# Weight sums moved from GpSimd to VectorE, four planned latencies and half of the embedding evictions changed in a one-core encoder layer

## The chip, the core and the metric

One of the eight cores of a Trainium2 chip runs the whole layer as one program. The engines that matter are TensorE (PE in the profile; its weight loads are listed apart as PEld), VectorE (DVE), ScalarE (ACT), GpSimd (POOL) and SyncE (SP), which issues all DMA transfers of this kernel. Each engine works through its own list of instructions in order and waits on semaphores. The metric is the device time of one execution in microseconds (us).

## The reference, cut to what matters

```python
def layer(x, p, pre_g, w_in, sink, ln_g, ln_b, ws, bs, w_out, post_g, w_pe, w_pg):
    h = rms_norm(x, pre_g)
    z = h @ w_in                                    # 2048 -> 5632
    q, k, v, g_attn, u, vg, g_gmlp = jnp.split(z, IN_SPLITS, axis=-1)
    q, k = rope(q), rope(k)
    a = window_attention(q, k, v, sink) * jax.nn.silu(g_attn)
    m = spatial_gating(gelu(u), gelu(vg), ln_g, ln_b, ws, bs) * jax.nn.silu(g_gmlp)
    y = jnp.concatenate([a, m], axis=-1) @ w_out    # 2048 -> 2048
    x = x + rms_norm(y, post_g)
    return x + jax.nn.sigmoid(x @ w_pg) * (p @ w_pe)
```

It is applied to two sequences of 1024 and 512 tokens, 1536 tokens together, in float32.

## The kernel before

**Products.** The three large products are cut into five sweeps: "a", "b" and "c" make the columns of w_in, "y" those of w_out, "p" those of w_pg. A sweep takes the 1536 tokens in two halves of 768 and the 2048 inputs in two halves of 1024, and multiplies by Strassen's scheme: seven products, in the order 3, 5, 7, 1, 4, 2, 6 (`ORDER`), stand for eight. Product `pr` of weight tile `i` is one pass of TensorE: 8 operand tiles times 2 column blocks of 384 times 3 matmuls. The 3 are there because every float32 value is split in two parts that TensorE takes at full rate, a high part (a copy by ScalarE) and a low part (a difference by VectorE), and high*high, high*low and low*high are added up (`mm3`, lines 174 to 176). There are 266 passes.

**What a pass needs.** For five of the seven products the weight of a pass is a sum or difference of two quarters of the weight matrix. `make_weights` loads both quarters (SyncE, into pool `wrp` of four buffers), adds them on GpSimd (lines 155 and 158 are the helpers `add` and `sub` that record the instruction), and `split_to` makes the high part on ScalarE (line 166) and the low part on VectorE (line 158). Such a sum is 128x1024 elements; there are 190. Names are built alike: `wra4_7` is the raw weight quarter (wr) of sweep a, product 4, tile 7, and `wta4_7` the split weight (wt) made of it; the profile drops the numbers. The operands are `ar` (raw), `a` (split): `ara`, `aa` in sweep a, `arc`, `ac` in sweep c. `psa` to `psp` are the PSUM tiles of the passes, two banks-pairs that take turns, so pass i+2 can start only when pass i has been taken out. `leave_product` takes a pass out of PSUM and adds it to the running outputs `u`, `v`, `o`, on VectorE and ScalarE. At the end of one product the eight operands of the next are split, one after another, while the last pass runs.

**Beside the passes.** `embed` multiplies p by w_pe first (16 tiles j, two halves h, PSUM tiles `pspe`); `leave_pe` copies each out on VectorE (line 397) and stores it. Meanwhile x is squared and summed (`accx`, `sq`) for the first norm, and the first operands are made of it (`x0_normed`, line 440). `rope` turns q and k with three multiplications, one of them on GpSimd, and an addition on GpSimd. `attention` runs 12 blocks of tokens times 2 groups of heads one after another between the matmuls of sweeps b and c: `attend_qk` splits q and k (`qs`, `ks`), the scores are taken (`s`), VectorE and ScalarE make the probabilities `p`, `turn` transposes them (`t`) and splits them (`pt`), `weigh` multiplies them with `vs` (`o`).

**What sets the order.** Nothing is decided on the chip. The program is recorded by a planner (`Line`): each job is a generator that records some instructions and yields how many microseconds it expects until its next step can run; the planner's clock advances with the matmuls recorded (0.1733 us each), and a step is recorded when it is due. So a number behind `yield` says how many matmuls are recorded between one step and the next. A number that is too small puts an instruction in its engine's list before its input is there, and the engine waits.

Of the kernel before, what the change touches and what calls it, by code (L numbers as in the profile page):

```python
# [11 lines left out]
AF = mybir.ActivationFunctionType  # L12
# [11 lines left out]
CH = HT // 2  # L24
# [69 lines left out]
def when(done):  # L94
    while not done():
        yield 0.5
# [3 lines left out]
def tile_encoder_layer(ctx: ExitStack, tc: tile.TileContext, xT, pT, wall, pre_g, post_g, sink,  # L100
                       ln_g, ln_b, wsT, bs, cos, sin, mask, out):
    nc = tc.nc
# [19 lines left out]
    def work(name):  # L122
        return wk.tile([P, HT], F32, tag="wk", name=name)

    def four(name, shape=None, dt=F32):
        return s4p.tile(shape or [P, 1024], dt, tag="s4", name=name)
# [5 lines left out]
    def banks(name):  # L132

        return psm.tile([P, 2, T], F32, tag="ps", name=name)

    def side(name):
        return pss.tile([P, T], F32, tag="sd", name=name)
# [4 lines left out]
    def load(dst, src):  # L142
        nc.sync.dma_start(out=dst, in_=src)
# [10 lines left out]
    def add(eng, o, a, b):  # L154
        eng.tensor_tensor(out=o, in0=a, in1=b, op=ALU.add)  # L155

    def sub(eng, o, a, b):
        eng.tensor_tensor(out=o, in0=a, in1=b, op=ALU.subtract)  # L158
# [4 lines left out]
    V, G = nc.vector, nc.gpsimd  # L163

    def split_to(src, hi, lo, us=1.2):
        nc.scalar.activation(hi, src, AF.Copy)  # L166
        yield us
        sub(V, lo, src, hi.bitcast(F32))

    def halves(t):  # L170
        return t.rearrange("p (c x) -> p c x", c=2)

    def mm3(ps, l, r, start, stop, us):
        nc.tensor.matmul(ps, lhsT=l[0], rhs=r[0], start=start, stop=False)  # L174
        nc.tensor.matmul(ps, lhsT=l[0], rhs=r[1], start=False, stop=False)  # L175
        nc.tensor.matmul(ps, lhsT=l[1], rhs=r[0], start=False, stop=stop)  # L176
        line.spend(3 * us)
# [18 lines left out]
    def load_w(dst, f, h):  # L196

        if f[0] == "c":
            load(dst, wall[f[1], :, h * 1024:(h + 1) * 1024])
            return  # L200
        for i in range(2):
            src = wall[f[1] + 2 * h + i].rearrange("p (k n) -> p k n", k=4)
            load(dst[:, i * 512:(i + 1) * 512].rearrange("p (k n) -> p k n", k=4),
                 src[:, :, f[2]:f[2] + P])
# [10 lines left out]
    def make_weights(j, sw, pr, i):  # L215

        nm = f"{sw.name}{pr}_{i}"
        sign, *quarters = B_OF[pr]
        rs = []
        for kh, n in quarters:  # L220
            r = wrp.tile([P, 1024], F32, tag="wr", name=f"wr{nm}_{n}{kh}")
            load_w(r, sw.pairs[i][n][0], kh)
            rs.append(r)
        yield 9.0
        if sign:
            (add if sign > 0 else sub)(G, rs[0], rs[0], rs[1])
            yield 3.5
        yield from when(lambda: passes[0] >= j - 2)
        w = wtp.tile([P, 2, 1024], F32R, tag="wt", name=f"wt{nm}")
        yield from split_to(rs[0], w[:, 0, :], w[:, 1, :])  # L230
        weights[j] = w
# [162 lines left out]

    def leave_pe(j, h, ps):
        o = arp.tile([P, HT], F32, tag="ar", name=f"pe{j}_{h}")
        V.tensor_copy(out=halves(o), in_=ps[:, :, 0:CH])
        yield 1.6
        store(pe_d[j][h], o)

# [174 lines left out]
    def span_of(n):  # L575
        lo, hi = (0, 8) if n < 8 else (8, 12)
        return max(lo, n - 1), min(hi, n + 2)

    def attend_qk(g, n, into):
        b0, b1 = span_of(n)  # L580
        w = (b1 - b0) * P
        nm = f"{g}_{n}"
        h, off = n // HB, (n % HB) * P
        r = [work(f"aq{nm}"), work(f"ak{nm}")]
        load(r[0][:, 0:512].rearrange("p (i t) -> p i t", i=4),
             q_d[g][h][:, :, off:off + P].rearrange("i p t -> p i t"))
        load(r[1][:, 0:w], k_d[g][:, b0 * P:b1 * P])
        yield 9.0
        q = four(f"qs{nm}", [P, 2, 512], F32R)
        ks = four(f"ks{nm}", [P, 2, 512], F32R)  # L590
        nc.scalar.activation(q[:, 0, :], r[0][:, 0:512], AF.Copy)
        nc.scalar.activation(ks[:, 0, 0:w], r[1][:, 0:w], AF.Copy)
        yield 0.8
        sub(V, q[:, 1, :], r[0][:, 0:512], q[:, 0, :].bitcast(F32))
        yield 0.6
        sub(V, ks[:, 1, 0:w], r[1][:, 0:w], ks[:, 0, 0:w].bitcast(F32))
        yield 3.0
        into.append((q, ks))

    def attend_v(g, n, into):  # L600
        b0, b1 = span_of(n)
        w = (b1 - b0) * P
        nm = f"{g}_{n}"
        r = work(f"av{nm}")
        load(r[:, 0:w].rearrange("p (b d) -> p b d", b=b1 - b0), v_d[g][b0:b1].rearrange("b p d -> p b d"))
        yield 9.0
        vs = four(f"vs{nm}", [P, 2, 512], F32R)
        yield from split_to(r[:, 0:w], vs[:, 0, 0:w], vs[:, 1, 0:w], 0.8)
        yield 0.8
        into.append(vs)  # L610

    def attend(g, n, got):

        b0, b1 = span_of(n)
        m0 = (b0 - n + 1) * P
        nb = b1 - b0
        w = nb * P
        nm = f"{g}_{n}"
        h, off = n // HB, (n % HB) * P
        yield from when(lambda: got)  # L620
        q, ks = got.pop()
        mx = small.tile([P, 4], F32, tag="mx", name=f"mx{nm}")
        sm = small.tile([P, 4], F32, tag="sm", name=f"sm{nm}")
        es = small.tile([P, 4], F32, tag="es", name=f"es{nm}")
        gv = []
        line.spawn(attend_v(g, n, gv), 1.0)
        ss, ps_ = [], []

        def reduce(i):
            hd = 4 * g + i  # L630
            p = pp.tile([P, 3 * P], F32, tag="p", name=f"p{nm}_{i}")
            V.tensor_tensor_reduce(out=p[:, 0:w], in0=ss[i][:, 0:w], in1=mask_sb[:, m0:m0 + w],
                                   op0=ALU.add, op1=ALU.min, scale=-SCALE,
                                   scalar=nsink[:, hd:hd + 1], accum_out=mx[:, i:i + 1])
            ps_.append(p)

        def expo(i):
            nc.scalar.activation(ps_[i][:, 0:w], ps_[i][:, 0:w], AF.Exp, scale=-1.0, bias=mx[:, i:i + 1],
                                 accum_out=sm[:, i:i + 1])

        for i in range(6):
            if i < 4:
                ss.append(side(f"s{nm}_{i}"))
                mm3(ss[i][:, 0:w], [q[:, x, i * P:(i + 1) * P] for x in range(2)],
                    [ks[:, x, 0:w] for x in range(2)], True, True, w / 2400. + 0.0133)
            if 1 <= i < 5:
                reduce(i - 1)
            if i >= 2:
                expo(i - 2)
            yield 1.0  # L650
        add(V, es, mx, sink_sb[:, 4 * g:4 * g + 4])
        yield 0.3
        nc.scalar.activation(es, es, AF.Exp)
        yield 0.6
        add(V, sm, sm, es)
        V.reciprocal(out=sm, in_=sm)
        yield 0.6
        for i in range(4):
            nc.scalar.activation(ps_[i][:, 0:w], ps_[i][:, 0:w], AF.Copy, scale=sm[:, i:i + 1])
        yield 4.6  # L660
        pts = {}

        def turn(b):
            tp = side(f"t{nm}_{b}")
            for i in range(4):
                nc.tensor.transpose(tp[:, i * P:(i + 1) * P], ps_[i][:, b * P:(b + 1) * P], ident)
            line.spend(0.43)
            yield 0.4
            pt = pts[b] = four(f"pt{nm}_{b}", [P, 2, 512], F32R)
            yield from split_to(tp, pt[:, 0, :], pt[:, 1, :], 0.9)  # L670

        def weigh(b):
            mm3(o, [vs[:, x, b * P:(b + 1) * P] for x in range(2)],
                [pts[b][:, x, :] for x in range(2)], b == 0, b == nb - 1, 0.2266)

        yield from turn(0)
        yield from turn(1)
        yield from when(lambda: gv)
        vs = gv[0]
        yield 2.0  # L680
        o = side(f"o{nm}")
        weigh(0)
        if nb > 2:
            yield from turn(2)
            yield 2.0
        for b in range(1, nb):
            weigh(b)
        yield 0.8
        t = work(f"ao{nm}")
        nc.scalar.activation(t[:, 0:512], o, AF.Copy)  # L690
        yield 1.5
        store(at_d[g][h][:, :, off:off + P].rearrange("i p t -> p i t"),
              t[:, 0:512].rearrange("p (i t) -> p i t", i=4))
        attended.add((g, n))
# [193 lines left out]
    pq.clear()  # L888
    embedded.append(True)
    line.spawn(make_weights(2, *items[2]))  # L890

    j = 0
    for s, (sw, pr) in enumerate(segs):
        n = len(sw.pairs)
        out_of = {5: (1, 0), 4: (0, 0), 2: (0, 1), 6: (1, 1)}.get(pr)
        for i in range(n):
# [12 lines left out]
            ps = banks(f"ps{sw.name}{pr}_{i}")  # L909
# [86 lines left out]
```

## Time and profile before

| | us |
|---|---|
| time, median of 3 runs | 2557.67 (2557.42 to 2560.88) |
| profiled execution, own time | 2555.26 |
| its span, first to last instruction | 2553.5 |
| TensorE busy | 2483.7 (97%) |
| VectorE busy | 1731.8 (68%) |
| ScalarE busy | 966.0 (38%) |
| GpSimd busy | 708.1 (28%) |
| mean granted TensorE clock | 0.992 |

TensorE is busy for 97% of the span and idle for 69.8 us of it. Busy time alone doesn't tell what a change of the other engines is worth: it is to be read from the waits of TensorE, one by one, and from what held the engine that ended each of them.

### The profile page before, as it was taken

To read this page: it belongs to the slowest core of one execution; us is meant where nothing else is said; L and a number is where in the kernel's file an instruction comes from. 1 tells how busy PE (TensorE), PEld (TensorE's weight loads), DVE (VectorE), ACT (ScalarE), POOL (GpSimd) and SP (SyncE) were. 2 spreads that over 40 slices of the span, in tenths; PEclk is the share of its full clock that TensorE was granted. 3 is DMA by queue.
4 is the path that set the end of the run, shared out by engine and by line. 5 is a ranking of instruction groups with operands and counts; after the bars stand their busy time and mean duration, and the time that the engine had idled before them with its cause. 6 is when DMAs were issued, how large, how long until landed. Compare 5 with 4: busy or idle time off the path is not lost.

```text
span 2553.5 us, 36547 instructions
## 1 busy us (share of the span) xinstructions
PE 2483.7 (97%) x14268; PEld 2448.7 (96%) x14268; DVE 1731.8 (68%) x1903; ACT 966.0 (38%) x1386; POOL 708.1 (28%) x300
## 2 busy tenths in 40 slices
PE   7999999999999999999998899999999999999999
PEld 7898999999989999999998899999999999999998
DVE  7659566866676767667767665556577976757775
ACT  3243222224775543333546742332233333322421
POOL 0254334454022102301221013203220331433444
PEclk9999999999999999999999999999999999999999
DMA  8957776667566688878656577567577988879985
GB/s 292 387 197 262 249 238 230 225 211 263 195 225 212 180 270 293 303 248 300 200 173 209 187 273 280 219 215 250 170 245 257 342 313 305 302 251 301 325 315 208
DMA packets 372397, 645.97 MB, mean 253 GB/s; under 512 B 29312, under 2 KB 212096, under 8 KB 372224
## 3 DMA queue, kind: packets, MB, share of 16 engines
q1 hardware_dynamic: 372224, 643.63, 73.9%
q8 instruction: 112, 1.84, 0.3%
q14 instruction: 61, 0.50, 0.1%
HBM read 533.43 MB, written 110.10 MB: 252 GB/s over the span
## 4 chain that ended last, share of the span: by engine, by line
PE 80%; DVE 9%; ACT 4%; issue 3%; DMA 3%; POOL 1%; SPq 1%; DVEq 0%; POOLq 0%; ACTq 0%
PE psy L175 6%; PE psy L176 6%; PE psy L174 6%; PE psp L175 6%; PE psp L176 6%; PE psp L174 6%; PE psc L176 4%; PE psc L174 4%; PE psc L175 4%; PE psa L175 4%; PE psa L176 4%; PE psa L174 4%; PE psb L175 4%; PE psb L176 4%; PE psb L174 4%
## 5 line engine op out<-in xcount | busy, mean ns | idle before, releaser
L174 PE MATMUL psa<-aa,wta 128*128 128x384 f32 x896 | 302.3, 337 | 5.7 <-DVE oa L155 3.8
L175 PE MATMUL psa<-aa,wta 128*128 128x384 f32 x896 | 301.7, 337 | 6.0 <-DVE aa L158 5.9
L176 PE MATMUL psa<-aa,wta 128*128 128x384 f32 x896 | 301.1, 336 | 5.8 <-DVE wta L158 5.8
L174 PE MATMUL psc<-ac,wtc 128*128 128x384 f32 x896 | 305.5, 341 | 0.0
L174 PE MATMUL psp<-ap,wtp 128*128 128x384 f32 x896 | 300.5, 335 | 3.2 <-ACT ap L166 2.6
L175 PE MATMUL psp<-ap,wtp 128*128 128x384 f32 x896 | 300.5, 335 | 2.4 <-DVE ap L158 2.4
L175 PE MATMUL psc<-ac,wtc 128*128 128x384 f32 x896 | 301.4, 336 | 0.3 <-DVE ac L158 0.3
L176 PE MATMUL psc<-ac,wtc 128*128 128x384 f32 x896 | 300.7, 336 | 0.0
L176 PE MATMUL psp<-ap,wtp 128*128 128x384 f32 x896 | 299.9, 335 | 0.0
L174 PE MATMUL psy<-ay,wty 128*128 128x384 f32 x896 | 299.6, 334 | 0.0
L176 PE MATMUL psy<-ay,wty 128*128 128x384 f32 x896 | 299.3, 334 | 0.0
L175 PE MATMUL psy<-ay,wty 128*128 128x384 f32 x896 | 299.3, 334 | 0.0
L174 PE MATMUL psb<-ab,wtb 128*128 128x384 f32 x672 | 231.2, 344 | 0.5 <-DVE ua L155 0.5
L175 PE MATMUL psb<-ab,wtb 128*128 128x384 f32 x672 | 226.4, 337 | 2.7 <-DVE ab L158 2.7
L176 PE MATMUL psb<-ab,wtb 128*128 128x384 f32 x672 | 226.0, 336 | 0.0
L175 PEld LDWEIGHTS psa<-aa,wta 128*128 128x128 f32 x896 | 169.3, 189 | 8.4 <-DVE aa L158 8.3
L174 PEld LDWEIGHTS psa<-aa,wta 128*128 128x128 f32 x896 | 169.5, 189 | 6.7 <-issue 4.1
L176 PEld LDWEIGHTS psa<-aa,wta 128*128 128x128 f32 x896 | 169.5, 189 | 6.1 <-DVE wta L158 6.1
L174 PEld LDWEIGHTS psp<-ap,wtp 128*128 128x128 f32 x896 | 168.6, 188 | 4.0 <-ACT ap L166 2.9
L175 PEld LDWEIGHTS psp<-ap,wtp 128*128 128x128 f32 x896 | 168.7, 188 | 3.9 <-DVE ap L158 3.6
L175 PEld LDWEIGHTS psc<-ac,wtc 128*128 128x128 f32 x896 | 169.2, 189 | 1.6 <-DVE ac L158 1.0
L174 PEld LDWEIGHTS psc<-ac,wtc 128*128 128x128 f32 x896 | 169.5, 189 | 0.5
(257 smaller groups left out, 5429.8 us busy)
## 6 DMA issues: line engine op xcount, KB each, us to landing
wrc<-wall SPq DMA_DIRECT2D x96, 512.0 KB, 6.5
arb<-h SPq DMA_DIRECT2D x96, 384.0 KB, 5.9
arc<-h SPq DMA_DIRECT2D x96, 384.0 KB, 6.0
wry<-wall SPq DMA_DIRECT2D x72, 512.0 KB, 6.2
wrp<-wall SPq DMA_DIRECT2D x72, 512.0 KB, 6.8
arp<-x SPq DMA_DIRECT2D x88, 384.0 KB, 6.5
wra<-wall SPq DMA_DIRECT2D x60, 512.0 KB, 5.9
ara<-h SPq DMA_DIRECT2D x80, 384.0 KB, 5.9
```

Of the source, the lines that this page charges most:

```text
L174: nc.tensor.matmul(ps, lhsT=l[0], rhs=r[0], start=start, stop=False)
L175: nc.tensor.matmul(ps, lhsT=l[0], rhs=r[1], start=False, stop=False)
L176: nc.tensor.matmul(ps, lhsT=l[1], rhs=r[0], start=False, stop=stop)
```

## The change

Three things are changed. The sum of two weight quarters is recorded on VectorE instead of GpSimd, with a planned latency of 1.6 us instead of 3.5. Four planned latencies in the attention are longer: after the split of k, 4.0 instead of 3.0; after the scaling of the probabilities, 5.6 instead of 4.6; before each of the two groups of `weigh`, 3.2 instead of 2.0. And `leave_pe` takes half h=0 out of PSUM on ScalarE, half h=1 on VectorE as before.

```diff
@@ make_weights
         yield 9.0
         if sign:
-            (add if sign > 0 else sub)(G, rs[0], rs[0], rs[1])
-            yield 3.5
+            (add if sign > 0 else sub)(V, rs[0], rs[0], rs[1])
+            yield 1.6
         yield from when(lambda: passes[0] >= j - 2)
@@ leave_pe
-        V.tensor_copy(out=halves(o), in_=ps[:, :, 0:CH])
+        if h:
+            V.tensor_copy(out=halves(o), in_=ps[:, :, 0:CH])
+        else:
+            nc.scalar.activation(halves(o), ps[:, :, 0:CH], AF.Copy)
         yield 1.6
@@ attend_qk
         sub(V, ks[:, 1, 0:w], r[1][:, 0:w], ks[:, 0, 0:w].bitcast(F32))
-        yield 3.0
+        yield 4.0
         into.append((q, ks))
@@ attend
             nc.scalar.activation(ps_[i][:, 0:w], ps_[i][:, 0:w], AF.Copy, scale=sm[:, i:i + 1])
-        yield 4.6
+        yield 5.6
...
         vs = gv[0]
-        yield 2.0
+        yield 3.2
         o = side(f"o{nm}")
         weigh(0)
         if nb > 2:
             yield from turn(2)
-            yield 2.0
+            yield 3.2
```

Since the latencies set the order, instructions move. On VectorE, at the first passes of sweep a (product 3, tiles 2 and 3; `ara5_0` and `ara5_1` are sums of operands of the next product), the list of before (-) and of now (+):

```order
 L158 TENSOR_TENSOR aa3_6_1060<-x0_6_345,aa3_6_1060 128x768
+L158 TENSOR_TENSOR wra3_2_10_1042<-wra3_2_10_1042,wra3_2_11_1044 128x1024
 L155 TENSOR_TENSOR ara5_0_00_1065<-ara5_0_00_1065,ara5_0_01_1067 128x768
+L158 TENSOR_TENSOR wra3_3_10_1076<-wra3_3_10_1076,wra3_3_11_1078 128x1024
+L158 TENSOR_TENSOR wta3_2_1159<-wra3_2_10_1042,wta3_2_1159 128x1024
+L158 TENSOR_TENSOR wta3_3_1171<-wra3_3_10_1076,wta3_3_1171 128x1024
 L155 TENSOR_TENSOR ara5_1_00_1101<-ara5_1_00_1101,ara5_1_01_1103 128x768
-L158 TENSOR_TENSOR wta3_2_1173<-wra3_2_10_1042,wta3_2_1173 128x1024
-L158 TENSOR_TENSOR wta3_3_1184<-wra3_3_10_1076,wta3_3_1184 128x1024
```

The two sums have come in, and the low parts of both weights now stand ahead of the sum `ara5_1` instead of behind it.

On GpSimd before, in sweep a, product 4 (`oa` is an output of q; `cos` and `rbq` are the multiplication and the addition of the rotation):

```order
L161 TENSOR_TENSOR oa_4_3654<-oa_4_3654,cos 128x768
L158 TENSOR_TENSOR wra_6_01_3596<-wra_6_01_3596,wra_6_00_3599 128x1024
L155 TENSOR_TENSOR oa_4_3654<-oa_4_3654,rbq_0_3669 128x768
L161 TENSOR_TENSOR oa_4_3728<-oa_4_3728,cos 128x768
L158 TENSOR_TENSOR wra_7_01_3673<-wra_7_01_3673,wra_7_00_3676 128x1024
L155 TENSOR_TENSOR oa_4_3728<-oa_4_3728,rbq_0_3743 128x768
```

And on VectorE now, at the same place:

```order
L155 TENSOR_TENSOR oa_4_3728<-va_2033,psa_4_3650 128x768
L155 TENSOR_TENSOR ara_6_10_3660<-ara_6_10_3660,ara_6_11_3662 128x768
L161 TENSOR_TENSOR rbq_0_3743<-oa_4_3728,sin 64x768 x2
L158 TENSOR_TENSOR wra_7_01_3673<-wra_7_01_3673,wra_7_00_3676 128x1024
L158 TENSOR_TENSOR wta_7_3766<-wra_7_01_3673,wta_7_3766 128x1024
L155 TENSOR_TENSOR oa_4_3798<-va_2111,psa_5_3724 128x768
```

The weight sums have left GpSimd's list, where they stood behind the multiplications of the rotation, and stand on VectorE directly ahead of the low part that uses them.

## Rows read from the trace of the kernel before

**Rows 1.** Page, part 1: busy us (share of the span) and instructions of each engine.

```profile
PE 2483.7 (97%) x14268; PEld 2448.7 (96%) x14268; DVE 1731.8 (68%) x1903; ACT 966.0 (38%) x1386; POOL 708.1 (28%) x300
```

**Rows 2.** Waits of TensorE: us in total, times, longest us.

```profile
PE o L175 <- DVE pt L158: 8.0, 5, 3.9
PE t L666 <- ACT p L659: 7.7, 20, 1.8
...
PE psa L175 <- DVE aa L158: 5.9, 5, 2.3
PE pspe L174 <- DVE pe L397: 5.9, 3, 3.3
...
PE s L175 <- DVE ks L158: 5.3, 5, 1.8
...
PE psb L175 <- DVE ab L158: 2.7, 3, 1.7
...
PE o L174 <- ACT pt L166: 2.2, 1, 2.2
```

**Rows 3.** Groups by line: names, shapes, count | busy, mean ns | idle before.

```profile
L155 POOL TENSOR_TENSOR wry<-wry,wry 128x1024 f32<-128x1024 f32 x24 | 65.2, 2719 | 231.1 <-DMA wry<-wall 151.0 <-DVE oy L155 73.4 <-DVE vy L158 6.7
...
L155 POOL TENSOR_TENSOR wrb<-wrb,wrb 128x1024 f32<-128x1024 f32 x18 | 44.3, 2462 | 207.3 <-DMA wrb<-wall 177.6 <-DVE ub L155 9.3 <-DMA gm<-gu 7.8
...
L155 DVE TENSOR_TENSOR vy<-vy,psy 128x768 f32<-128x768 f32 x16 | 15.2, 952 | 40.1 <-PE psy L176 40.1
```

**Rows 4.** Timelines of 50 to 62 us: start, us, instruction, idle before and releaser.

```profile
53.90 2.83 POOL L158 TENSOR_TENSOR wra<-wra,wra 128x1024 f32<-128x1024 f32 x1 [9.84 <-DMA wra<-wall]
54.41 3.14 DVE L158 TENSOR_TENSOR aa<-x,aa 128x768 fp32r<-128x768 f32 x1
57.48 1.21 DVE L158 TENSOR_TENSOR wtpe<-wrpe,wtpe 128x1024 fp32r<-128x1024 f32 x1
59.61 0.69 PE L174 MATMUL pspe<-pa,wtpe 128*128 128x384 f32 x1 [3.29 <-DVE pe L397]
```

**Rows 5.** Timelines of 98 to 118 us.

```profile
110.13 2.36 POOL L158 TENSOR_TENSOR wra<-wra,wra 128x1024 f32<-128x1024 f32 x1 [5.33 <-DMA wra<-wall]
114.02 1.41 DVE L155 TENSOR_TENSOR ara<-ara,ara 128x768 f32<-128x768 f32 x1 [7.55 <-DMA ara<-h]
115.35 3.97 DVE L158 TENSOR_TENSOR wta<-wra,wta 128x1024 fp32r<-128x1024 f32 x2
116.62 0.69 PE L176 MATMUL psa<-aa,wta 128*128 128x384 f32 x1 [5.79 <-DVE wta L158]
```

**Rows 6.** Timelines of 422 to 446 us.

```profile
437.18 2.39 POOL L158 TENSOR_TENSOR wra<-wra,wra 128x1024 f32<-128x1024 f32 x1
443.35 0.81 ACT L280 ACTIVATE va<-psa 128x768 f32<-128x768 f32 x1 [2.69 <-DVE oa L155]
444.21 0.44 PE L174 MATMUL psa<-aa,wta 128*128 128x384 f32 x1 [1.89 <-ACT va L280]
```

**Rows 7.** Timelines of 232 to 258 us.

```profile
233.31 2.60 DVE L440 SCALAR_TENSOR_TENSOR xb<-xb,pre_sb,rb_x 128x768 f32<-128x768 f32 x1
242.75 0.66 PE L174 MATMUL psa<-aa,wta 128*128 128x384 f32 x1 [3.84 <-DVE oa L155]
257.15 0.44 PE L175 MATMUL psa<-aa,wta 128*128 128x384 f32 x1 [2.28 <-DVE aa L158]
```

**Rows 8.** Eight stretches by window: us, busy (count) of each engine, granted clock, DMA.

```profile
594.20:597.60 3.40, 3.23 (x10) 3.23 (x11) 3.40 (x5) 3.40 (x6) 0.16 (x1) 0.50 1.01 372
...
sum 37.40, PE 30.14 PEld 29.44 DVE 33.05 ACT 22.08 POOL 7.96; mean PE 3.77 PEld 3.68 DVE 4.13 ACT 2.76 POOL 1.00
```

**Rows 9.** Timelines of 1344 to 1362 us.

```profile
1351.91 4.00 DVE L158 TENSOR_TENSOR ac<-arc,ac 128x768 fp32r<-128x768 f32 x2
1352.70 2.40 POOL L158 TENSOR_TENSOR wrc<-wrc,wrc 128x1024 f32<-128x1024 f32 x1 [4.59 <-DMA wrc<-wall]
1358.30 0.50 PE L175 MATMUL o<-pt,vs 128*128 128x512 f32 x1 [3.86 <-DVE pt L158]
```

**Rows 10.** Waits of all engines, GpSimd on the weights' loads: total, times, longest.

```profile
POOL wrb L155 <- DMA wrb<-wall: 177.6, 13, 70.6
```

## The prediction

> **What bounds the kernel now.** I read the busy times first: TensorE has work for 2483.7 us, VectorE for 1731.8, ScalarE 966.0, GpSimd 708.1 [rows 1]. The span is 2553.5 us, so TensorE is idle for 69.8 us, and no change that leaves its matmuls alone can win more than these, plus what the clock loses. So the second view is the list of TensorE's waits, with the instruction that ended each [rows 2]. They are many and short. Those that the change can reach are of two kinds: waits of the attention's matmuls (o, t, s: 8.0 + 7.7 + 5.3 + 2.2 = 23.2 us), and waits of the sweeps and of the embedding for an operand or for a free PSUM bank (psa, psb, pspe). Third come the groups and timelines of GpSimd and VectorE around the waits [rows 3 to 7, 9], to see what held the engine that ended them. Fourth, the windows at the lower clock: behind the longer waits the granted clock is 0.50, that is 1.2 of 2.4 GHz, in eight stretches of together 37.40 us in which TensorE is busy for 30.14 [rows 8]. Half of that busy time, 15.1 us, is what this clock costs at most, 1.9 us for a stretch.
>
> **Part 1, the sums, as load.** 190 sums leave GpSimd and come to VectorE. On GpSimd one takes 2462 to 2719 ns [rows 3]. On VectorE a two-input operation of the same 128x1024 elements takes 1.21 us [rows 4], so 190 x 1.21 = 230 us are added. Against that stands a stretch that now goes: while GpSimd's sum runs (53.90, for 2.83), VectorE's `aa` of 768 elements takes 3.14 us [rows 4]; of the same size but with one input in PSUM it takes 0.952 [rows 3], and two `ac` beside GpSimd's `wrc` take 4.00 [rows 9]. So a GpSimd sum that meets such an operation costs VectorE up to 3.14 - 0.95 = 2.19 us. If each of the 190 met one, VectorE would lose 416 us of stretch, if none, nothing; I take 1 us for each, 190, since GpSimd is busy 28% of the span with pauses between and many of its sums meet operations with a PSUM input. VectorE then comes to 1731.8 + 230 - 190, about 1770 us (ends 1546 and 1962), GpSimd to about 708 - 190 x 2.6 = 210. VectorE stays below TensorE by over 500 us even at the upper end. As load the move costs nothing; what it is worth hangs on the places where TensorE waits.
>
> By the Trainium skill (SBUF — State Buffer, Who interferes with whom) GpSimd and a VectorE instruction with two inputs in SBUF exclude each other, whichever comes first, and one with a single SBUF input isn't touched; the 3.14 beside 0.952 agrees. The rule also speaks against the change: a moved sum has two SBUF inputs, so GpSimd's remaining multiplications and additions of the rotation can hold it, as they hold other VectorE work now. By the rule the sum below would come out some 2 us worse (an estimate).
>
> **Part 1, the places.** (a) *Embedding, 50 to 62 us.* `aa` loses its 2.19 us of stretch, and `wtpe` and the copy `pe` behind it on VectorE come that much earlier; TensorE's 3.29 there [rows 4] shrinks by **2.2**. (b) *Sweep a begins, 98 to 118 us.* Before, both low parts stand behind `ara5_1`, whose load lands at 114.02, and TensorE goes on at 116.62, when the first low part is done. Now they stand ahead of it. The second sum's load lands at 110.13 [rows 5]; the sum (1.21) and the first low part (1.21) then end at 112.55. So **4.1** of 5.79 go, 1.7 stay. VectorE waits for that load too, idle as it is since 106.47 (114.02 less 7.55). (c) *232 to 258 us.* TensorE waits 3.84 and 2.28 behind a stretched chain on VectorE [rows 7], 6.1 together. One of its links, `xb` with 2.60 where 0.95 would do, is beside a multiplication of the rotation, which stays on GpSimd, so its 1.65 stay: **4.5** go. (d) *Sums between the rotation's steps.* At 437.18 a sum holds GpSimd for 2.39 while the rotation's addition waits behind it; `va` waits for `oa` and TensorE 1.89 for `va` [rows 6]. At the start of sweep b it is the same with `ab`: 2.7 in three waits [rows 2]. Both go, **4.6**. (e) *At 1358.30* TensorE waits 3.86 for `pt` behind the two `ac` that take 4.00 instead of 1.90 [rows 9]; of this 2.1 the sum that now runs on VectorE takes 1.2 back: **0.9**.
>
> **Part 1, what it adds.** A sum on VectorE waits for its load, and the low parts and exits queued behind it wait too. On GpSimd it held up little: its idle time before `wry` and `wrb` is mostly a wait for exactly these loads (151.0 of 231.1, 177.6 of 207.3) [rows 3], one of them 70.6 us long [rows 10]. The planned distance between load and sum is unchanged, and VectorE comes to its own instructions later than an idle GpSimd does, so most loads should have landed. One that has not is in rows 5: VectorE would stand 3.7 us (106.47 to 110.13). Nothing in the trace prices this: none of VectorE's waits is for a weight's load. Bounds: 0 if the few late ones hit VectorE ahead of its need, and the 68 us of rival B. I take **+5.9**, as much again as the waits for `aa` amount to now, the row of the same kind (an operand late on VectorE) [rows 2]. The shorter latency of 1.6 against 3.5 fits 1.21 us and costs nothing unless the sum is held.
>
> **Part 2, the latencies.** 1.0 us more ahead of the scores and of the transposes, 1.2 more ahead of each `weigh`: about 6 or 7 more matmuls of the running sweep stand in TensorE's list ahead of the waiting one. No work is added. Every wait falls by the margin at most. Taken wait by wait: s 5.3 in 5, falls by 4.1; t 7.7 in 20, by 5.5; o behind the low part 8.0 in 5 (longest 3.9), by 3.9; o behind the high part 2.2 in 1, by 1.2 [rows 2]: **14.7**. The ends are 0, if the whole chain shifts and waits as before, and the 23.2 of all. A block's chain gets 1.0 + 1.0 + 1.2 (+ 1.2) longer, up to 4.4 us; the blocks run one after another beside sweeps that last hundreds of us, so it is hidden while the last block still ends before its output is wanted; if not, the planner would record it early and TensorE would wait there.
>
> **Part 3, embedding evictions.** 16 of 32 copies go from VectorE to ScalarE, which does a 768-column exit of PSUM in 0.81 us [rows 6] and is busy for 38% of the span. 16 x 0.81 = 13 us lie beside other work. The gain is in (a); of the 5.9 of pspe the rest stays, since I see nothing that frees it. Bounds -3 to +2.
>
> **Clock.** Stretches at 0.50 go with the waits ahead of them. Of eight I count two and a half gone (a wait that stays behind at 1.7 may still leave one), 2.5 x 1.9 = **4.7**; ends 0 and 15.1.
>
> **The sum.** -2.2 - 4.1 - 4.5 - 4.6 - 0.9 + 5.9 - 14.7 - 4.7 = -29.8. From the profiled execution's own 2555.26 that is 2525.5. The median of the runs shown is 2.4 above it, so the forecast is 2527.9, and I say 2528.
>
> **Rivals.** *A, no change:* waits are moved, not taken away; each block of the attention is late by as much elsewhere, and VectorE's waits for loads eat (a) to (e): 2553 to 2562. For it: TensorE is at 97% [rows 1], so it is easy to give back 1%. Against it: the waits in rows 2 have named causes on an engine that is lightened at just these places. The Trainium skill (Perfetto Trace Analysis, Identifying the Most-Contended Engine) says to improve the busiest engine first; by it, nothing would come of this change. The trace bears that out only as far as 69.8 us is all there is.
> *B, slower:* VectorE, in order, stands before each weight's load, and at the product boundaries, where eight operands are split and nothing may slip, TensorE waits for it. There are 34 boundaries; two late sums at each by 1 us make 68 us, against the 30 above: 2558 + 68 - 30 = 2596. It decides once the loads land some 4 us later, against VectorE's turn, than at 110.13 now. For it: rows 10. Against it: with 210 instead of 708 us GpSimd stretches VectorE less, and VectorE still idles 30%.
> *C, more:* all the waits named go whole (23.2 + 3.3 + 5.8 + 6.1 + 4.6, some 43), with 12 of the clock's 15.1: -55, 2503.
> *D, less:* the attention's waits reappear behind other links of their chain (14.7 becomes 0): -15 and 2543.
>
> **How the numbers follow.** Forecast, 2515 to 2537: 0.56. C 0.12. D 0.13. A 0.12. B 0.07. About 0.2%, 5.1 us, is what a measurement of this kernel can tell from no change. Faster by more: 0.56 + 0.12 + 0.13 = 0.81; within: 0.12; slower: 0.07. The range leaves out B, most of A and the far end of C: 2506 to 2553.
>
> **What the profile will show.** If right: VectorE about 1770, GpSimd about 210; TensorE's idle time from 69.8 to about 45; no wait for `va` near 444 and none of 2 us at sweep b's start; some 1.7 us at the first weight near 112; the attention's waits together about 8; short waits of VectorE for `wr` loads; an `aa` of 0.95 beside no sum. Rival A shows the same loads but TensorE's idle time at 65 to 70, B long waits of VectorE for `wr` followed by TensorE's for `aa`, `ab`, `ac`, `ay`. The forecast is wrong if VectorE's waits for loads sum to tens of us on the chain that ended last, or if the lists at the boundaries put sums ahead of exits that TensorE needs.

## The result, and the profile after

The changed kernel takes 2499.83 us (median of 4 runs, 2497.27 to 2501.20), the kernel before 2557.55 (4 runs): a ratio of 0.9771, 95% interval 0.9754 to 0.9787. It is 57.7 us faster. The forecast was 30 us and 2528; the range began at 2506. The sign was right and the gain almost twice as large.

The profiled execution of the changed kernel has a span of 2499.4 us, 54.1 less than before. Busy time of the engines (page, part 1; it answers to [rows 1]):

```profile
PE 2463.5 (99%) x14268; PEld 2439.0 (98%) x14268; DVE 1777.5 (71%) x2077; ACT 980.6 (39%) x1400; POOL 225.3 (9%) x110
```

VectorE and GpSimd are where the prediction put them (1770 and 210). TensorE's idle time fell from 69.8 to 2499.4 - 2463.5 = 35.9 us, that is by 33.9; the forecast was 25.1. Its busy time fell too, by 20.2 us with the same 14268 matmuls, where I had expected 4.7.

Waits of TensorE after (us in total, times, longest; they answer to [rows 2]):

```profile
...
PE pspe L174 <- ACT pe L400: 3.5, 2, 2.5
PE psa L174 <- DVE oa L155: 3.5, 1, 3.5
PE psa L176 <- DVE wta L158: 3.4, 1, 3.4
PE o L175 <- DVE pt L158: 2.5, 3, 1.4
PE psa L175 <- DVE aa L158: 2.1, 2, 1.3
PE o L174 <- ACT pt L166: 2.0, 2, 1.1
PE pspe L174 <- DVE pe L398: 1.6, 3, 0.6
PE psp L174 <- ACT ap L166: 1.2, 1, 1.2
...
PE psp L175 <- DVE ap L158: 0.5, 1, 0.5
PE s L175 <- DVE ks L158: 0.5, 1, 0.5
PE psb L175 <- DVE ab L158: 0.3, 1, 0.3
PE t L669 <- ACT p L662: 0.2, 1, 0.2
```

The attention's four waits, 23.2 us before, are 2.5 + 2.0 + 0.5 + 0.2 = 5.2. Every wait for an operand of the sweeps shrank, and no wait for `va` is left. In the embedding the waits for `pe` (line 397 before) are now split between the copies of ScalarE (L400) and of VectorE (L398), 3.5 + 1.6 against 5.9. VectorE does wait for weights' loads now, as expected, some 30 us in sum; the largest row of its waits is this:

```profile
DVE wra L158 <- DMA wra<-wall: 10.6, 5, 7.0
```

Timelines after, at the places of [rows 4], [rows 5] and [rows 7] (start, us, instruction, idle before and releaser):

```profile
56.59 0.95 DVE L158 TENSOR_TENSOR aa<-x,aa 128x768 fp32r<-128x768 f32 x1
```
```profile
55.80 0.44 PE L174 MATMUL pspe<-pa,wtpe 128*128 128x384 f32 x1 [0.60 <-DVE pe L398]
```
```profile
107.46 1.23 DVE L158 TENSOR_TENSOR wra<-wra,wra 128x1024 f32<-128x1024 f32 x1 [2.25 <-DMA wra<-wall]
108.60 2.43 DVE L158 TENSOR_TENSOR wta<-wra,wta 128x1024 fp32r<-128x1024 f32 x2
```
```profile
109.87 0.69 PE L176 MATMUL psa<-aa,wta 128*128 128x384 f32 x1 [3.44 <-DVE wta L158]
...
235.84 0.66 PE L174 MATMUL psa<-aa,wta 128*128 128x384 f32 x1 [3.52 <-DVE oa L155]
```

`aa` takes 0.95 instead of 3.14 us, and TensorE's wait there is 0.60 instead of 3.29. At the first weight VectorE waits 2.25 for the load, adds, and makes the low part at once, but the load lands later against TensorE than before, so 3.44 of the wait stay where I had 1.7. In a second profile of the same kernel ("changed, again" below) this wait is 2.0:

```profile
PE psa L176 <- DVE wta L158: 2.0, 1, 2.0
```

At 236 us the wait of 3.84 is still 3.52; only the later one of 2.28 is gone. The moved sum has itself come into the chain ahead of it: beside the rotation's multiplication on GpSimd it takes 2.87 us instead of 1.23, and `xb` behind it still takes 2.60 (VectorE and GpSimd, after):

```profile
227.43 2.87 DVE L155 TENSOR_TENSOR wra<-wra,wra 128x1024 f32<-128x1024 f32 x1
230.23 2.60 DVE L443 SCALAR_TENSOR_TENSOR xb<-xb,pre_sb,rb_x 128x768 f32<-128x768 f32 x1
```
```profile
226.75 2.48 POOL L161 TENSOR_TENSOR oa<-oa,cos 128x768 f32<-128x768 f32 x1 [5.77 <-PE psa L176]
```

Stretches with the granted clock at 0.50 (the 1.2 GHz level) after, and the sum of all (columns as in [rows 8]; the line before the sum is a single stretch):

```profile
109.43:112.84 3.41, 2.97 (x9) 2.97 (x10) 3.11 (x3) 2.38 (x4) 2.13 (x1) 0.50 1.04 415
...
sum 13.65, PE 11.83 PEld 11.28 DVE 12.93 ACT 10.70 POOL 2.13; mean PE 3.94 PEld 3.76 DVE 4.31 ACT 3.57 POOL 0.71
```

I had counted eight such stretches before; there are nine (the one at 34 us was left out), 40.95 us with TensorE busy for 33.59:

```profile
sum 40.95, PE 33.59 PEld 32.77 DVE 36.62 ACT 22.15 POOL 7.98; mean PE 3.73 PEld 3.64 DVE 4.07 ACT 2.46 POOL 0.89
```

Three are left. By half of TensorE's busy time in them the clock gives back (33.59 - 11.83) / 2 = 10.9 us.

### The profile page after: what moved, and what is told of

It is laid out like the page before. It is cut to its first block, busy times and chain, and to the rows that moved or that the text cites. A ratio compares the mean times of both kernels' runs of the same rounds, so it can differ in the third digit from the quotient of the medians.

```text
span 2499.4 us, 36241 instructions
## 1 busy us (share of the span) xinstructions
PE 2463.5 (99%) x14268; PEld 2439.0 (98%) x14268; DVE 1777.5 (71%) x2077; ACT 980.6 (39%) x1400; POOL 225.3 (9%) x110
## 4 chain that ended last, share of the span: by engine, by line
PE 90%; DVE 4%; ACT 2%; issue 1%; DMA 1%; SPq 0%; DVEq 0%; ACTq 0%
PE psp L174 6%; PE psp L176 6%; PE psp L175 6%; PE psy L176 6%; PE psy L175 6%; PE psy L174 6%; PE psc L175 6%; PE psc L174 6%; PE psc L176 6%; PE psa L176 5%; PE psa L175 5%; PE psa L174 5%; PE psb L176 4%; PE psb L174 4%; PE psb L175 4%; PE t L669 1%
```

## The experiments

All times are medians. The ratio is to the kernel before, measured beside each kernel on the same chip, where it took 2554.8 to 2560.4; so kernels that were not measured side by side are compared by ratio. "Span" is that of the profiled execution.

| kernel | us | ratio (95%) | span |
|---|---|---|---|
| changed kernel | 2499.83 | 0.9771 (0.9754 to 0.9787) | 2499.4 |
| sums alone | 2516.85 | 0.9833 (0.9810 to 0.9856) | 2515.4 |
| latencies alone | 2538.58 | 0.9919 (0.9899 to 0.9940) | 2535.6 |
| evictions alone | 2556.53 | 0.9988 (0.9973 to 1.0003) | 2551.4 |
| sums alone, latency 3.5 | 2519.83 | 0.9845 (0.9823 to 0.9868) | 2518.5 |
| changed, GpSimd adding idly | 2530.44 | 0.9889 (0.9870 to 0.9907) | 2528.5 |
| changed, rotation on VectorE | 2495.47 | 0.9755 (0.9739 to 0.9772) | 2493.9 |
| changed, loads 6.0 ahead | 2524.07 | 0.9868 (0.9852 to 0.9884) | 2521.4 |
| changed without evictions | 2500.46 | 0.9772 (0.9757 to 0.9787) | 2499.7 |
| changed, again | 2499.99 | 0.9783 (0.9763 to 0.9803) | 2497.7 |
| rotation, loads 11.0 ahead | 2502.57 | 0.9788 (0.9770 to 0.9807) | 2500.3 |
| rotation and output on VectorE | 2498.25 | 0.9769 (0.9749 to 0.9788) | 2497.4 |
| sums alone, GpSimd adding idly | 2549.34 | 0.9962 (0.9948 to 0.9976) | 2543.8 |

Two theories stood against each other. Theory 1: each part takes away the waits that the prediction gave it. Theory 2: GpSimd's work stretched VectorE all over the kernel, so the sums are worth much more than the stalls that the prediction named, and the attention's waits were partly theirs.

### Each part alone

```diff
-            (add if sign > 0 else sub)(G, rs[0], rs[0], rs[1])
-            yield 3.5
+            (add if sign > 0 else sub)(V, rs[0], rs[0], rs[1])
+            yield 1.6
```

> The kernel before with the 190 sums on VectorE and the latency of 1.6 us, attention latencies and evictions as before. Theory 1 (each part takes away its own waits): the waits of sweeps a, b and p for operands, weights and exits fall by some 16 us, the embedding's by 2, the clock gives back about 6: 24 us faster, 2534; the attention's waits for t, s and o stay near 23 us. Theory 2 (the stretch of VectorE beside GpSimd made the attention's waits too): its waits for ks and pt fall by half as well, about 38 us faster, 2520. Rival B of the prediction (VectorE blocked by loads) would show as less than 10 us.

It is 43.5 us faster, more than theory 2 gave. Waits of TensorE in this kernel:

```profile
PE pspe L174 <- DVE pe L397: 7.4, 6, 2.7
PE t L666 <- ACT p L659: 4.9, 17, 1.0
PE o L175 <- DVE pt L158: 4.0, 4, 1.6
PE o L174 <- ACT pt L166: 4.0, 2, 3.8
...
PE s L175 <- DVE ks L158: 0.8, 1, 0.8
```

With no latency touched, the attention's waits have fallen from 23.2 to 13.7 us, those for `ks` from 5.3 to 0.8. A place in the kernel before shows how. VectorE's low part of a weight meets GpSimd's sum of another and takes 3.44 us instead of 1.21; `ks`, which the scores want, stands behind it, and TensorE waits (timeline of the kernel before, 1389 to 1394 us, VectorE, GpSimd and TensorE):

```profile
1389.51 3.44 DVE L158 TENSOR_TENSOR wtc<-wrc,wtc 128x1024 fp32r<-128x1024 f32 x1 [0.59 <-ACT wtc L166]
```
```profile
1389.47 2.40 POOL L158 TENSOR_TENSOR wrc<-wrc,wrc 128x1024 f32<-128x1024 f32 x1 [11.98 <-DMA wrc<-wall]
```
```profile
1393.47 0.44 PE L175 MATMUL s<-ks,qs 128*128 128x384 f32 x1 [1.79 <-DVE ks L158]
```

The prediction had read this 1.79, the longest of the waits for `ks`, as a latency planned too short.

In the embedding the sums alone made it worse: the waits for `pe` rose from 5.9 to 7.4. The one of 3.29 is down to 1.10, but three more of 1.44, 0.31 and 1.41 follow within 11 us. VectorE's list has no pause there, and the sum of 1.22 us stands in it just ahead of a copy `pe`.

The latencies alone:

```diff
-        yield 3.0
+        yield 4.0
...
-        yield 4.6
+        yield 5.6
...
-        yield 2.0
+        yield 3.2
...
-            yield 2.0
+            yield 3.2
```

> The kernel before with the four attention latencies alone. Theory 1: the waits for t, s and o fall from 23 to about 6 us, the short waits between t's matmuls that count as busy time go too, some 7 us, and two or three stretches at the lower clock: 27 us faster, 2530. Theory 2: as the stretch of VectorE stays, waits of 1 to 4 us for pt and ks stay: 12 to 15 us faster, 2544. If the waits reappear at other links (rival D), under 5 us.

21.7 us faster, between the two. The waits for `ks` are gone and those of t fall to 1.5, but those of o behind the low part stay, and those for `ab` rise from 2.7 to 5.8:

```profile
PE o L175 <- DVE pt L158: 7.4, 5, 2.5
PE psb L175 <- DVE ab L158: 5.8, 5, 2.2
```

From this kernel to the changed one the span falls by another 36.2 us. That is what the sums bring on top of the latencies, since the evictions are not told from nothing (below). TensorE's idle time has 22.7 of it: 5.6 in the attention's waits, 5.5 in those for `ab`, 3.6 in those for `ap`, the rest in smaller ones. The other 13.5 are in its busy time.

The evictions alone:

```diff
-        V.tensor_copy(out=halves(o), in_=ps[:, :, 0:CH])
+        if h:
+            V.tensor_copy(out=halves(o), in_=ps[:, :, 0:CH])
+        else:
+            nc.scalar.activation(halves(o), ps[:, :, 0:CH], AF.Copy)
```

> The kernel before with the embedding's evictions by turns on ScalarE and VectorE alone. Theory 1: the wait of 2.2 us at 31 us is a load's and stays, the one of 3.3 at 56 us loses 1 to 2 because the copy no longer stands behind the stretched low part: 0 to 3 us faster, 2555 to 2558. If ScalarE, with the high parts in its list, is late for the evictions: 1 to 4 us slower.

3.8 us by the medians, an interval that reaches 1: not told from nothing. Taken out of the changed kernel they are worth nothing either:

```diff
-        if h:
-            V.tensor_copy(out=halves(o), in_=ps[:, :, 0:CH])
-        else:
-            nc.scalar.activation(halves(o), ps[:, :, 0:CH], AF.Copy)
+        V.tensor_copy(out=halves(o), in_=ps[:, :, 0:CH])
```

> The changed kernel with all evictions of the embedding on VectorE as before. If the evictions are worth what they are alone: 3 to 4 us slower than the changed kernel. If sums on VectorE make its list in the embedding longer, so that the evictions on ScalarE are worth more there: 5 to 8 us slower. If they are worth nothing: within 2 us.

0.9772 against 0.9771. This run also gives the latencies on top of the sums: from 0.9833 to 0.9772, 0.0061 of 2557.55 = 15.6 us, by the two intervals some 9 to 23. The three parts alone add up to 69 us, together they bring 57.7; sums and latencies overlap in the attention's waits.

### Which engine adds, or how early the low part stands

```diff
-            (add if sign > 0 else sub)(G, rs[0], rs[0], rs[1])
+            (add if sign > 0 else sub)(V, rs[0], rs[0], rs[1])
             yield 3.5
```

> As the first of these kernels (sums on VectorE alone), but with the old latency of 3.5 us behind the sum. If what matters is the engine that adds: within 3 us of the first kernel. If the gain comes from the low parts standing earlier in VectorE's list (at 110 us ahead of the next operand's sum): the wait of 5.8 us for wta at 110 us comes back in part and the kernel is 4 to 8 us slower than the first.

3 us by the medians, intervals that overlap. The wait for `wta` is 5.3 here and 2.3 with 1.6. With the old order at the first weights it is 4.2 to 7.4 (before, latencies alone, evictions alone), with the new one 1.0 to 3.4 (sums alone, changed twice, changed without evictions). So place (b) of the prediction is real, but of the gain the move of the sums to VectorE makes nearly all.

### GpSimd busy with work that nobody reads

```diff
             (add if sign > 0 else sub)(V, rs[0], rs[0], rs[1])
+            add(G, rs[1], rs[1], rs[1])
             yield 1.6
```

> The changed kernel, and behind each sum on VectorE GpSimd adds the second quarter, which is spent, to itself in place: 190 additions of the old size on GpSimd, whose result nobody reads; no weight waits for them. Theory 2 (GpSimd's work stretches VectorE): VectorE's busy time rises from 1777 by 150 us or more although its list is the same, waits of TensorE for pt, ks and aa come back, 15 to 30 us slower than the changed kernel. Theory 1 (it was the weights and the rotation standing in GpSimd's list): only the rotation stands behind these additions again, and a buffer is held 2.4 us longer: 2 to 6 us slower.

30 us slower than the changed kernel. No weight waits for these additions, VectorE's waits for the weights' loads are 35 us instead of 30, its work is the same, and it is busy for 172 us more:

```profile
PE 2474.0 (98%) x14268; PEld 2439.8 (96%) x14268; DVE 1949.4 (77%) x2077; ACT 979.1 (39%) x1400; POOL 660.8 (26%) x300
```

0.9 us for each of the 190 additions. Of the 29.1 us by which the span is longer, 18.6 are idle time of TensorE and 10.5 its busy time. The waits that come back are mostly those at the product boundaries (TensorE, the kernel with idle additions):

```profile
PE psa L175 <- DVE aa L158: 5.7, 8, 1.3
PE psa L174 <- DVE oa L155: 5.2, 1, 5.2
PE psp L175 <- DVE ap L158: 5.2, 6, 1.8
...
PE psb L175 <- DVE ab L158: 3.3, 4, 1.2
```

The attention's waits did not come back as expected; with the longer latencies they stay at 2.7 + 2.0 + 0.5 + 0.4 = 5.6. Of theory 1 little is seen: no wait for `va` has returned, and the one for `oa` is 1.7 longer.

One of the waits from start to end, on VectorE, GpSimd and TensorE. `ap` takes 2.47 beside GpSimd's addition, 0.95 elsewhere in the same list:

```profile
2051.85 2.47 DVE L158 TENSOR_TENSOR ap<-x,ap 128x768 fp32r<-128x768 f32 x1
```
```profile
2050.14 3.36 POOL L155 TENSOR_TENSOR wrp<-wrp 128x1024 f32<-128x1024 f32 x1 [11.09 <-DVE wrp L158]
```
```profile
2054.37 0.69 PE L175 MATMUL psp<-ap,wtp 128*128 128x384 f32 x1 [1.81 <-DVE ap L158]
```

The same addition put into the kernel with the sums alone:

```diff
             (add if sign > 0 else sub)(V, rs[0], rs[0], rs[1])
+            add(G, rs[1], rs[1], rs[1])
             yield 1.6
```

> The kernel with the sums on VectorE alone (attention latencies and evictions as before), and behind each sum GpSimd adds the spent second quarter to itself, 190 additions that nobody reads. Theory 2 (the attention's waits for ks and pt come in large part from VectorE's stretch beside GpSimd): the waits for ks, which fell from 5.3 to 0.8 us with the sums, come back to 3 us or more, those for pt behind the low part from 4.0 to 6 or more; 0.993 of the kernel before, 2535 to 2545, that is 20 to 30 us slower than the sums alone. Theory 1: the attention's waits stay as with the sums alone, and the kernel is 3 to 8 us slower than that, 2520 to 2525.

0.9833 becomes 0.9962, 33 us by the ratios, 28.3 by the spans, where theory 2 asked for 20 to 30. Where it lands is not as expected, though; `ks` and `pt` stay short of the 3 and 6 us that were asked:

```profile
PE pspe L174 <- DVE pe L398: 9.7, 7, 3.2
...
PE o L175 <- DVE pt L158: 5.4, 4, 1.9
...
PE t L667 <- ACT p L660: 5.1, 17, 1.1
...
PE o L174 <- ACT pt L166: 4.0, 2, 3.8
...
PE s L175 <- DVE ks L158: 2.8, 2, 1.4
```

The attention's waits rise only from 13.7 to 17.3, not towards 23.2; the rest is again in the operands and the embedding. The idle additions follow VectorE's sum, while the real ones began when their loads landed, so they meet other operations: VectorE's 280 low parts of the sweeps' operands take 321.9 us in the kernel before, 276.9 with the sums alone and 292.4 here, its 271 low parts of weights 396.8, 363.5 and 451.4. An idle addition, whose two inputs are one tensor, is also shorter, 1.89 us undisturbed against 2.36 [rows 5]. How the 9.5 us that the sums took off the attention divide between stretch and the changed order stays open beyond these 3.6.

### Loads nearer and farther

```diff
-        yield 9.0
+        yield 6.0
         if sign:
             (add if sign > 0 else sub)(V, rs[0], rs[0], rs[1])
```

> The changed kernel with the sum recorded 6.0 us behind the loads of its quarters instead of 9.0; these loads take about 6 to 7 us from issue to landing. Rival B of the prediction (a VectorE that stands before each late load makes TensorE wait): VectorE waits for wr loads nearly 190 times and TensorE behind it, 20 us or more slower than the changed kernel. My theory (VectorE idles 29% of the span and works ahead of TensorE): its waits for loads rise to over 100 us in sum, but the time by less than 8 us.

About 25 us slower than the changed kernel by the ratios: rival B's mechanism exists. VectorE's waits for `wr` loads rise from 30 to 204 us in sum. One of them, on VectorE and TensorE: the sum waits 5.69 for its load, an exit, two operations and `ks` stand behind it, and the scores wait.

```profile
1184.05 1.23 DVE L155 TENSOR_TENSOR wrc<-wrc,wrc 128x1024 f32<-128x1024 f32 x1 [5.69 <-DMA wrc<-wall]
```
```profile
1188.13 0.51 PE L175 MATMUL s<-ks,qs 128*128 128x384 f32 x1 [2.78 <-DVE ks L158]
```

My own expectation, under 8 us, was wrong: with 174 us more of waiting the span is 22 longer. VectorE's busy time fell at the same time (1777.5 to 1742.1) and the order of its list changed, so the 22 are a net figure and no price for each microsecond of waiting.

### The rotation on VectorE, and two steps further

```diff
-            mul(G, o[:, s:e], o[:, s:e], c)
+            mul(V, o[:, s:e], o[:, s:e], c)
...
-        add(G, o, o, b)
+        add(V, o, o, b)
```

> The changed kernel with the rotation's last multiplication and its addition on VectorE too. Theory 2: each pair on GpSimd now takes 2.6 + 2.7 us and stretches two VectorE operations by 1.6 us each; on VectorE the pair takes about 1.9. The waits of 3.5 and 1.3 us at 232 us and the lower clock behind them (6.8 us long) go: 4 to 8 us faster than the changed kernel, 2492 to 2496. Theory 1 (only what stands in a list counts): VectorE's list gets about 40 us longer in sweep a, where it is already late: 0 to 5 us slower than the changed kernel.

0.9755 against 0.9771 and 0.9783 of the changed kernel, measured twice: 4 to 7 us faster, but the intervals overlap. The profile shows what moved. TensorE's longest wait of the sweep (3.5 for `oa`) is down to 0.3:

```profile
PE psa L174 <- DVE oa L155: 0.3, 1, 0.3
```

and VectorE's busy time rises by 3 us only (1777.5 to 1780.8), although 50 operations came to it: the stretch that they took away pays for them.

> The changed kernel itself, as the measure for the two beside it on the same chip: 0.977 of the kernel before, 2498 to 2503.

```diff
-        yield 9.0
+        yield 11.0
         if sign:
             (add if sign > 0 else sub)(V, rs[0], rs[0], rs[1])
```

> The changed kernel with the rotation on VectorE, and the sums recorded 11.0 us behind their loads instead of 9.0. If VectorE's remaining waits for these loads (30 us in sum) cost TensorE at the rate that 6.0 showed (174 us more of them made it 22 us slower): 3 to 4 us faster than the rotation on VectorE alone, 0.974 of the kernel before, 2490 to 2493. If the four buffers are too few for loads so early, the DMA queue stands before them and the operands' loads behind slip: 5 us or more slower than the rotation alone, 2500 or above.

0.9788, slower than the rotation alone. VectorE's waits for these loads fall from 29 us to 11, but at the first weights the order is the old one again: the low part stands behind the sum of the next operand, and that one waits for its load (VectorE and TensorE of this kernel):

```profile
110.71 1.51 DVE L155 TENSOR_TENSOR ara<-ara,ara 128x768 f32<-128x768 f32 x1 [2.63 <-DMA ara<-h]
```
```profile
PE psa L176 <- DVE wta L158: 5.8, 1, 5.8
```

TensorE is idle for 4.8 us more than with the rotation alone, and 3.4 of them are this wait (2.4 there). So it lost mainly by an order that came out worse; that the DMA queue stands before the buffers isn't shown.

```diff
-            add(G, o, o, x[:, 0:HT])
+            add(V, o, o, x[:, 0:HT])
```

> The changed kernel with the rotation and also the last additions of the output (31 operations of 2.2 us in sweep p) on VectorE, so that GpSimd is left with the first squares alone. If any stretch of VectorE costs TensorE at the rate of the kernel with idle sums (172 us more of VectorE's time made it 29 us slower): some 50 us of stretch go, 30 us of additions come, 2 to 4 us faster than the rotation alone. If only a stretch ahead of something that TensorE waits for costs: in sweep p no such wait is left but 2 us, within 2 us of the rotation alone.

0.9769, the same as the rotation alone (0.9755) within the intervals: that the stretch by the output's additions costs anything can't be told. It is not that sweep p bears any stretch: the idle additions, which meet its operands, brought the waits for `ap` from 0.5 to 5.2.

## Why the prediction was wrong

By its own steps, with the waits of the two profiles (us; what was not priced is marked so). The rows overlap by about 1 us (below) and leave out some small waits, so they don't add up to the 54.1 of the spans:

| step | predicted | measured |
|---|---|---|
| (a) embedding | -2.2 | -0.8 (all waits for `pe`, 5.9 to 3.5 + 1.6; at the place itself 3.29 to 0.60) |
| (b) first weight | -4.1 | -2.4 (5.8 to 3.4; by the second profile to 2.0) |
| (c) 232 to 258 us | -4.5 | -2.6 (2.28 gone, 3.84 to 3.52) |
| (d) behind GpSimd's sums | -4.6 | -4.3 (1.9 + 2.7 to 0.3) |
| (e) and the latencies: s, t, o | -15.6 | -18.0, and -5.5 of t's busy time |
| waits for `ap` | not priced | -3.3 (2.6 + 2.4 to 1.2 + 0.5) |
| new waits behind late loads | +5.9 | none beside the one in (b) |
| clock | -4.7 | -10.9 |

**What held.** The loads of the engines; that the load itself costs little, though in the embedding a sum stands ahead of a copy and TensorE waits; the order at the first weights; (d); the evictions, priced at nothing. The latencies, 14.7 against 15.6 measured on top of the sums, agree partly by luck: the 14.7 stood for the attention's waits alone, and on top of the sums these fell by 8.6 (13.7 to 5.1); most of the rest, 5.4, is TensorE's busy time.

**The step that failed is part 1, its places: what the stretch of VectorE is worth to TensorE.** Of the forecast's 29.8 us the sums had 15.1 (all but the latencies' 14.7, with the clock); alone they bring 43.5, on top of the latencies 36. I had the stretch right in size, 1 us for each sum, 190 in all: the changed kernel's VectorE has 237.6 us of sums more and 15.3 us of copies less and is busy for only 45.7 more, so some 177 went, 0.9 for each sum. But I then declared it worth only what five places showed, since VectorE stays far below TensorE, and looked at the long waits only. The named places were not priced too low: (a) to (d) gave 10.1 where I had 15.4. What I missed lies beside them, in waits of the attention that I had put down to latencies, in those for `ap`, and in the clock and the busy time behind them. The idle additions show the scale: 172 us of stretch are 29 us of TensorE's span, a sixth, 18.6 of them idle time, mostly in waits of up to 2 us at the product boundaries. They stretch other operations than the real sums did, so this is no exact price of the 177. A lower mean load does not make a stretch harmless, because VectorE has no slack where eight operands are split in a row.

By the Trainium skill (SBUF — State Buffer, Who interferes with whom) GpSimd and a VectorE instruction with two SBUF inputs exclude each other, and the one that started first keeps the other out; an instruction with one SBUF input stays clear only outside VectorE's two-port modes, a condition that the prediction left out. The runs agree on the first: `ap` 2.47 instead of 0.95 beside an addition that had begun, and 172 us more of VectorE's time for idle additions. The price that I drew from it against the change, some 2 us from the rotation's operations, has its row at 227.43: the moved sum is held for 1.6 us, in the chain ahead of the wait that stayed at 3.52. So (c) came short because I left `xb`'s stretch standing there and put the sum at nothing. With the rotation on VectorE this wait is 0.3 and the span 5.5 us shorter, though the interval doesn't settle that gain.

**The second miss is the +5.9.** VectorE's waits for loads came as described, 30 us of them, and TensorE noticed none but the one at the first weight; no other of its waits stands at the times of VectorE's. I took the price of another wait instead of asking what VectorE had to do next at those places. The kernel with nearer loads shows the scale: 174 us more of such waits, and a span 22 us longer.

**The third is the clock**, 10.9 for 4.7. I let two and a half of eight stretches go. Six of nine went, with waits that shrank ahead of them. Which wait leaves such a stretch isn't told by its length alone: 3.44 at 110 us does and so do two of 0.9 and 1.4 at 1401 us, while the 2.5 for `pe` leaves none in this profile; so the clock's term could only be given between its ends, 0 and 15.1, and the value taken was too near the lower one.

**And t's busy time.** 44.2 us of "busy" for 256 matmuls became 38.7. Pauses between matmuls that are too short to be listed as waits stand in busy time; I took them for work. About 1 us of the 5.5 is the clock's, since t ran for 2.1 us of the stretches at 0.50 before and for none after. Of the fall of 20.2 us in busy time, clock and t so make some 15.4; the remaining 4.8 lie spread over many lines and were not traced.

**The rivals.** C (2503) came nearest by its number, not by its reason: not all named waits went, but unnamed ones did. D and A fell with the latencies' 15.6. B did not occur, but its mechanism is real at a load distance of 6.0. In A, the Trainium skill (Perfetto Trace Analysis, Identifying the Most-Contended Engine) says only which engine to improve first; that nothing would come of this change was my own conclusion, and the runs refute it: TensorE waited for VectorE, and VectorE had been held by GpSimd. B's 2596 set its 68 us against a gain that already held the +5.9 for the same waits; by its own terms it was some 2590. Adding up: idle time fell by 33.9 and busy time by 20.2, together 54.1, the difference of the spans.

## What to carry to other kernels

An engine that is a third idle can still set the pace: measure what a neighbour's work adds to the duration of its operations, and get the scale of its price by running the neighbour's work with nobody waiting for it, not from the few long stalls that the trace names. Where an addition moves to an engine whose list serves TensorE, its load must land before its turn; 3 us less of distance cost some 25 us here, more than the latencies or the evictions brought alone. And when two parts of a change shorten the same waits, time each alone before giving a wait to one of them.

## What the runs showed of the hardware

The contention hits the one that comes second. In the kernel with the sums alone and idle additions, VectorE's `ks` and two more operations run undisturbed while GpSimd's addition takes 4.09 us instead of the 1.89 that the next one takes (GpSimd and VectorE):

```profile
855.74 4.09 POOL L155 TENSOR_TENSOR wrb<-wrb 128x1024 f32<-128x1024 f32 x1 [13.11 <-DVE wrb L158]
862.75 1.89 POOL L155 TENSOR_TENSOR wrb<-wrb 128x1024 f32<-128x1024 f32 x1 [2.92 <-DVE sm L155]
```
```profile
855.52 0.55 DVE L158 TENSOR_TENSOR ks<-ak,ks 128x384 fp32r<-128x384 f32 x1
855.99 0.95 DVE L158 TENSOR_TENSOR ab<-arb,ab 128x768 fp32r<-128x768 f32 x1
856.86 1.22 DVE L158 TENSOR_TENSOR wtb<-wrb,wtb 128x1024 fp32r<-128x1024 f32 x1
```

So an addition on GpSimd and an operand's low part on VectorE cost VectorE 1.5 us (`ap`, 2.47 instead of 0.95) or nothing (`ab`), by which engine holds the other out.

The clock adds to what removed waits bring: the changed kernel's 34 us less idle time came with 10.9 us from the granted clock, which was at 0.50 in nine stretches before and in three after.
